# Weight tiles of the first stage put into the chain of loads, a gate tile between the fold and the first pooled tile, and the second pair's norms through the forms' buffers

## The chip, the cores and the metric

The kernel runs on one core of a Trainium2 chip. The metric is the device time of one execution in microseconds; before the change it is 656.79 us, the median of three runs (655.18 to 657.51).

## The reference, cut to what matters

One layer of a pooling mixer over 2048 rows of 1024 channels, all in float32:

```
hn     = rms_norm(x, norm_g)
proj   = hn @ pool_w_in                      # split: u (768) | mq (256) | gate (1024)
tok    = (causal means of u over windows 2, 4, 8, 16, per group of 192, minus u) @ w_group * pool_scale
mem_o  = 4-head attention of mq over rms_norm(mem, mem_norm_g) @ w_mem_kv   # 256 memory rows
h      = x + (concat[tok, mem_o] * silu(gate)) @ w_out
out    = rms_norm(h, final_norm_g)
```

## The kernel before

Rows are worked on in two pairs of blocks of 512 rows: `s = 0` and `s = 1`. Every float32 product is made of three matmuls of a rounded high part and a remainder (`_mm3`, lines 51 to 53), so each weight tile is first split: a cast on ScalarE writes the high part `wh` (line 38), and a subtraction on VectorE the remainder `wl` (line 46). The matrix of the group mixing is folded into the input projection on the chip: `fold` writes the product to `w_z` in DRAM, eight transfers from line 323.

The first stage (`s = 0`) goes through the tiles of the list `TILES`: "q" tiles are memory queries, "g" tiles the gate, "z" tiles the pooled channels, whose weights come from `w_z`. One tile over both blocks is 48 matmuls of 512 columns, in four runs of 12; after each run `tile_in` calls `between`, which is a step counter. At numbered steps it fires hooks: the two row norms of the first pair (7 and 10), the fold and the loads of the memory (12 and 14), the memory's keys and values (17), `stats(0)` and `stats(1)`, which compute the row norms of the second pair, and `stage(k)` at 25, 34, 43 and 52, which builds the seven combinations ("forms") of the second pair's inputs that the second stage multiplies (a Strassen-like scheme with seven products for eight). At eighteen other steps it does a piece of the memory attention of the first pair: scores (lines 580 and 581), exponentials (587), transposes of the probabilities (603), and the mix with the values (615).

`stats(a)` (`row_stats`) loads four tiles of rows of 512 KB, squares and sums them on ScalarE (line 220, two row tiles a line of the program), takes the power on GpSimd (line 200), spreads the result over a 128x512 tile (line 207), transposes that by four matmuls against the identity (209), copies it out of PSUM (210) and writes one row of it to `rows` in DRAM (253). `stage(k)` reads `rows` back, broadcast over the partitions, into two tiles `s` (259), and scales the inputs with them (266). In the kernel before, the two tiles in `row_stats` come from the pool `sg`, which has two buffers; the gate tiles use the same pool on their way to DRAM (`sg`, lines 497 and 498) and when a pooled tile reads them back (line 514). The pool `st`, name `s`, has two buffers too; in the first stage it serves the fold's small weights and then only `stage`.

A pooled tile ends in `windows`: GpSimd adds shifted copies (line 522), VectorE finishes and multiplies with the gate (531 to 537), and the result goes to `br_d` (539). All its tiles are from the pool `zz`, four buffers, which the fold, the memory and `x_later` use as well. `x_later` runs at the end of the first stage: it brings four of the seven forms back from DRAM (289) and splits them into the buffers that held the first pair's inputs.

The weight tiles are 512 KB each, in four buffers `raw`. The order of instructions on each engine is set when the program is built, by a scheduler that simulates the engines; each engine then works strictly through its own list. Loads issued through the helper `load` keep their written order on SyncE's queue; a plain `sp.dma_start` goes where the scheduler puts it. Transfers issued by SyncE and by ScalarE take one of eight semaphores (`DMAHW0` to `DMAHW7`) in turn, and the instruction that issues a transfer waits for the last one on the same semaphore.

Of the kernel before, what the change touches and what calls it, by code (L numbers as in the profile page):

```python
# [8 lines left out]
F32 = mybir.dt.float32  # L9
# [6 lines left out]
P = 128  # L16
# [4 lines left out]
BT = 512  # L21
NB = S // BT
QT = BT // P
# [25 lines left out]
def _mm3(nc, ps, ahi, alo, bhi, blo, start, stop, **kw):  # L49

    nc.tensor.matmul(ps, lhsT=ahi, rhs=bhi, start=start, stop=False, **kw)  # L51
    nc.tensor.matmul(ps, lhsT=ahi, rhs=blo, start=False, stop=False, **kw)  # L52
    nc.tensor.matmul(ps, lhsT=alo, rhs=bhi, start=False, stop=stop, **kw)  # L53
# [3 lines left out]
def trunk(ctx, tc, x, xT, mem, memT, norm_g, mem_norm_g, w_mem, w_out, w_in, w_uT, w_g, p_scale, final_g,  # L57
# [10 lines left out]
    st = pool("st", 2)  # L68
# [3 lines left out]
    sgp = pool("sgp", 2)  # L72
# [7 lines left out]
    def raw_tile(shape=(P, D)):  # L80
        return raw.tile(list(shape), F32, name="raw")
# [46 lines left out]
    def load_rows_of(b, slots, how):  # L128

        rows = []  # L130
        for i in range(QT):
            if i % 2 == 0:
                t = slot(slots[i // 2], (P, 2, D), F32)
            rows.append(t[:, i % 2, :])
            how(out=rows[i], in_=x[b * BT + i * P:b * BT + (i + 1) * P, :])
        return rows
# [9 lines left out]
    def load_tile(w, how=sp.dma_start):  # L146
        wr = raw_tile((P, KT, P))
        how(out=wr, in_=w)
        return wr
# [11 lines left out]
    ahead = [wq0, load_tile(w_in[1], load)]  # L161
# [34 lines left out]
    def rstd_of(ssq, n):  # L196
        v = small.tile([P, QT], F32, name="var")
        nc.vector.tensor_scalar(v[:, :n], ssq, 1.0 / D, EPS, ALU.mult, ALU.add)
        r = small.tile([P, QT], F32, name="rstd")
        nc.gpsimd.tensor_tensor(out=r[:, :n], in0=v[:, :n], in1=half[:, :n], op=ALU.pow)  # L200
        return r

    def bcast_cols(r, n, dst):

        ps = (ps_t if n == QT else ps_mm).tile([P, BT], F32, name="pt" if n == QT else "mm")
        rb = sgp.tile([P, BT], F32, name="sg")[:, :n * P].rearrange("p (t f) -> p t f", t=n)
        nc.vector.tensor_copy(rb, r[:, :n].unsqueeze(2).broadcast_to([P, n, P]))
        for t in range(n):
            nc.tensor.matmul(ps[:, t * P:(t + 1) * P], lhsT=rb[:, t, :], rhs=ident, start=True, stop=True)
        nc.vector.tensor_copy(dst, ps[:, :n * P])  # L210
# [6 lines left out]
    def squares(rows):  # L217
        ss = small.tile([P, QT], F32, name="ss")
        for t in range(QT):
            nc.scalar.activation(out=rows[t], in_=rows[t], func=AF.Square, accum_out=ss[:, t:t + 1])  # L220
        return rstd_of(ss, QT)
# [26 lines left out]
    def row_stats(s, a, rows):  # L248

        r = load_rows_of(2 * s + a, (10 + 2 * a, 11 + 2 * a), load)  # L250
        rb = sgp.tile([P, BT], F32, name="sg")
        bcast_cols(squares(r), QT, rb)
        sp.dma_start(out=rows[a].rearrange("(o t) p -> o (t p)", o=1), in_=rb[0:1])

    def stage_forms(s, k, rows, X):
# [39 lines left out]
    w_z = dram.tile([NJ, P, KT, P], F32, name="w_z")  # L295
# [58 lines left out]
    def memory_norm(loaded):  # L354
        ssm = small.tile([P, 2], F32, name="ssm", bufs=1)
        for t in range(2):
            nc.scalar.activation(out=loaded[1][t], in_=loaded[1][t], func=AF.Square, accum_out=ssm[:, t:t + 1])
        loaded.append(rstd_of(ssm, 2))
# [44 lines left out]
    def chunk(src, hi_eng, shape=(P, BT), lo_eng="dve"):  # L403

        hi = ch.tile(list(shape), F32R, name="wh")
        lo = ch.tile(list(shape), F32R, name="wl")
        _split(nc, hi, lo, src, hi_eng, lo_eng)
        return hi, lo
# [48 lines left out]
    def tile_in(xs, wr, ws, take, between):  # L457


        ps = {a: ps_mm.tile([P, BT], F32, name="mm") for a in xs}  # L460
        for kh in range(2):
            if len(ws) <= kh:
                ws.append(chunk(wr[:, kh * KH:(kh + 1) * KH], "act", (P, KH, P)))
            hi, lo = ws[kh]
            for a, hl in xs.items():
                for k in range(KH):
                    _mm3(nc, ps[a], hi[:, k, :], lo[:, k, :], hl[kh][0][:, k, :], hl[kh][1][:, k, :], k + kh == 0,
                         kh == 1 and k == KH - 1)
                between()
        for a in xs:  # L470
            def scaled(a=a):
                take(0, a, ps[a], ALU.mult, norms[a])
            if a in norms:
                scaled()
            else:
                unscaled[a].append(scaled)
# [14 lines left out]
    def take_gate(s, j):  # L491
        def take(i, a, ps, op, rest):
            sg = sgp.tile([P, BT], F32, name="sg")
            if rest is not None:
                nc.vector.tensor_tensor(out=sg, in0=ps, in1=rest, op=op)
                ps = sg
            nc.scalar.activation(out=sg, in_=ps, func=AF.Silu)
            nc.scalar.dma_start(out=g_d[s][j + i, :, a, :], in_=sg)
        return take
# [226 lines left out]
    loaded = []  # L726
# [15 lines left out]
    def tile_of(s, kind, j, xs, between):  # L742
        if kind == "q":
            tile_in(xs, ahead[j], qws[j], take_query(s, j), between)
        elif kind == "g":
            tile_in(xs, ahead[7 - j] if j > 3 and j < 6 else load_tile(w_in[2 + j]), [], take_gate(s, j), between)
        else:
            tile_in(xs, load_tile(w_z[j]), [], take_pool(s, j), between)

    qws = [[], []]  # L750
    state = {}
# [2 lines left out]
    def stats(a):  # L754
        if not a:
            load(out=ci, in_=cinv)
            state["rows"] = dram.tile([2, QT, P], F32, name="rows")
        row_stats(1, a, state["rows"])

    def stage(k):  # L760
        if not X1:
            X1.update(x_slots((1, 6, 2)))
        stage_forms(1, k, state["rows"], X1)


    TILES = [("q", 0, (0,)), ("q", 1, (0,)), ("q", 0, (1,)), ("q", 1, (1,))]
    TILES += [(kind, j, (0, 1)) for kind, j in (("g", 5), ("g", 4), ("z", 5), ("g", 3), ("z", 4), ("g", 2), ("z", 3), ("g", 1),
                                                ("z", 2), ("g", 0), ("z", 1), ("z", 0), ("g", 6), ("g", 7))]

    def norm(a):  # L770
        first_norm(a)
        for f in unscaled[a]:
            f()

    hooks = {7: [lambda: norm(0)], 10: [lambda: norm(1)], 12: [fold, lambda: ahead.append(load_tile(w_in[6], load)), lambda: loaded.extend(load_memory())],
             14: [lambda: load_memory_rest(loaded)],
             15: [lambda: memory_norm(loaded)], 17: [lambda: memory(loaded)], 18: [lambda: stats(0)], 21: [lambda: stats(1)]}
    for k in range(KH):
        hooks[25 + 9 * k] = [lambda k=k: stage(k)]
    steps = Steps(0, 20, 2.5, hooks)  # L780
    xs = {0: first_block(0)}
    for kind, j, blocks in TILES:
        if 1 in blocks and 1 not in xs:
# [91 lines left out]
```

## Time and profile before

| | us |
|---|---|
| median of three runs | 656.79 |
| the profiled execution's own time | 654.72 |
| its span | 652.9 |
| TensorE busy with matmuls | 602.1 (92%) |
| VectorE busy | 408.8 (63%) |
| ScalarE busy | 326.9 (50%) |
| GpSimd busy | 152.7 (23%) |
| mean granted TensorE clock, share of full speed | 0.964 |

The page of the profile lists busy time and cuts the span into 40 slices. The timeline lists single instructions: start, duration, engine, line, what it writes and reads, and in brackets the idle time before it with what ended it. SPq and ACTq are the queues by which SyncE and ScalarE issue transfers. Matmuls overlap in the pipeline, so at full clock one of 512 columns is listed with 0.39 us and the next starts 0.23 us later.

### The profile page before, as it was taken

What the parts mean: (1) busy time and instruction counts of PE and PEld (TensorE: products, weight loads), DVE (VectorE), ACT (ScalarE), POOL (GpSimd) and SP (SyncE); (2) the same over time, 40 slices, a digit from 0 to 9 for tenths busy, and PEclk for the clock granted to TensorE, in tenths of its full rate; (3) what the DMA queues carried; (4) which work ended last, traced back from release to release, by engine and by line L of the source; (5) the groups of instructions that cost most, each with busy time, mean ns of one, the idle gap of its engine ahead of it and who ended that gap; (6) DMA issues with size and microseconds to landing.
All of it is one profiled execution on the core that took longest, in us unless ns stands there. A gap on an engine that the chain in (4) does not pass through costs nothing.

```text
span 652.9 us, 8411 instructions
## 1 busy us (share of the span) xinstructions
PE 602.1 (92%) x2846; PEld 500.7 (77%) x2846; DVE 408.8 (63%) x686; ACT 326.9 (50%) x674; POOL 152.7 (23%) x165
## 2 busy tenths in 40 slices
PE   8999619996999999999999899989999999999993
PEld 5789519884887788888888687868888888888882
DVE  6370314658878977687769866898883337615126
ACT  6735450435647574765864689742752324214112
POOL 0021022806150413000018400364000002206016
PEclk8999959996999999999999899998999999999998
DMA  8949990318668545656340732256894046950006
GB/s 317 400 154 333 402 353 20 107 42 261 227 212 293 204 173 185 203 174 207 119 146 8 234 122 99 94 188 216 318 406 178 32 148 216 358 214 0 1 0 258
DMA packets 54382, 124.41 MB, mean 191 GB/s; under 512 B 6722, under 2 KB 15682, under 8 KB 54340
## 3 DMA queue, kind: packets, MB, share of 16 engines
q1 hardware_dynamic: 45972, 106.57, 47.0%
q10 hardware_dynamic: 6832, 12.60, 5.2%
q0 software_dynamic: 1536, 4.72, 1.9%
q8 instruction: 22, 0.36, 0.2%
q14 instruction: 20, 0.16, 0.1%
HBM read 86.63 MB, written 36.70 MB: 189 GB/s over the span
## 4 chain that ended last, share of the span: by engine, by line
PE 66%; DVE 11%; DMA 8%; ACT 8%; issue 4%; SPq 1%; POOL 1%; ACTq 0%; POOLq 0%; DVEq 0%
PE mm L51 16%; PE mm L53 15%; PE mm L52 15%; PE sc L51 2%; PE sc L52 2%; PE pt L51 2%; PE pt L52 2%; PE sc L53 2%; PE pt L53 2%; DVE wl L46 2%; DVE zz L537 2%; ACT L587 2%; ACT pr L587 1%; PE sc L615 1%; DMA x<-in_x 1%
## 5 line engine op out<-in xcount | busy, mean ns | idle before, releaser
L51 PE MATMUL mm<-x,wh 128*128 128x512 f32 x480 | 191.4, 401 | 26.2 <-ACT wh L38 20.2
L52 PE MATMUL mm<-x,wh 128*128 128x512 f32 x480 | 190.4, 397 | 0.3 <-DVE x L229 0.3
L53 PE MATMUL mm<-x,wl 128*128 128x512 f32 x480 | 188.6, 398 | 0.1
L46 DVE TENSOR_TENSOR wl<-raw,wh 128x512 fp32r<-128x512 f32 x104 | 79.3, 767 | 102.7 <-ACT wh L38 100.8
L38 ACT CAST wh<-raw 128x512 fp32r<-128x512 f32 x104 | 63.5, 618 | 128.6 <-PE pt L53 74.2
L51 PEld LDWEIGHTS mm<-x,wh 128*128 128x128 f32 x480 | 92.1, 192 | 46.1 <-ACT wh L38 20.9
L522 POOL TENSOR_TENSOR zz<-zz 128x527 f32<-128x527 f32 (+6 forms) x64 | 82.2, 1297 | 162.0 <-ACT zz L547 78.0
L52 PEld LDWEIGHTS mm<-x,wh 128*128 128x128 f32 x480 | 92.2, 192 | 18.8 <-DVE x L229 0.6
L53 PEld LDWEIGHTS mm<-x,wl 128*128 128x128 f32 x480 | 91.8, 191 | 19.1 <-DVE wl L46 0.9
L52 PE MATMUL mm<-wl,x 128*128 128x512 f32 x128 | 49.8, 389 | 0.0
L51 PE MATMUL mm<-wh,x 128*128 128x512 f32 x128 | 49.6, 389 | 0.0
L53 PE MATMUL mm<-wh,x 128*128 128x512 f32 x128 | 49.6, 389 | 0.0
L674 POOL TENSOR_TENSOR rstdo<-sso,half 128x1 f32<-128x1 f32 x16 | 14.7, 919 | 129.6 <-DVE sso L716 129.6
L587 ACT ACTIVATE pr<-sc,nm 128x256 f32<-128x256 f32 x64 | 29.7, 470 | 22.3 <-DVE nm L583 16.4
L592 ACT ACTIVATE pr<-pr,rc 128x256 f32<-128x256 f32 x64 | 29.0, 502 | 11.0 <-DVE rc L590 10.5
L38 ACT CAST pth<-pt 128x512 fp32r<-128x512 f32 x32 | 18.7, 585 | 19.0 <-PE pt L603 14.2
L51 PEld LDWEIGHTS mm<-wh,x 128*128 128x128 f32 x128 | 24.0, 188 | 5.1
L52 PEld LDWEIGHTS mm<-wl,x 128*128 128x128 f32 x128 | 24.0, 188 | 5.0
L53 PEld LDWEIGHTS mm<-wh,x 128*128 128x128 f32 x128 | 24.0, 188 | 4.9
L38 ACT CAST x<-zz 128x512 fp32r<-128x512 f32 x32 | 18.2, 618 | 14.7 <-DMA zz<-br_d 7.1
L52 PE MATMUL sc<-wl,x 128*128 128x512 f32 x64 | 24.9, 389 | 0.0
L53 PE MATMUL sc<-wh,x 128*128 128x512 f32 x64 | 24.9, 389 | 0.0
(177 smaller groups left out, 1049.8 us busy)
## 6 DMA issues: line engine op xcount, KB each, us to landing
raw<-in_w_in SPq DMA_DIRECT2D x19, 512.0 KB, 4.9
x<-in_x SPq DMA_DIRECT2D x16, 512.0 KB, 8.7
g_d<-sg ACTq DMA_DIRECT2D x32, 256.0 KB, 2.9
raw<-in_w_out SPq DMA_DIRECT2D x16, 512.0 KB, 4.4
raw<-w_z SPq DMA_DIRECT2D x12, 512.0 KB, 3.9
sg<-g_d SPq DMA_DIRECT2D x24, 256.0 KB, 3.1
br_d<-zz SPq DMA_DIRECT2D x12, 512.0 KB, 3.5
x<-in_xT SPq DMA_DIRECT2D x8, 512.0 KB, 7.2
```

The lines of the kernel that those rows point to most:

```text
L38: return nc.scalar.copy(hi, src)
L46: return e.tensor_tensor(out=lo, in0=src, in1=hi.bitcast(F32), op=ALU.subtract)
L51: nc.tensor.matmul(ps, lhsT=ahi, rhs=bhi, start=start, stop=False, **kw)
L52: nc.tensor.matmul(ps, lhsT=ahi, rhs=blo, start=False, stop=False, **kw)
L53: nc.tensor.matmul(ps, lhsT=alo, rhs=bhi, start=False, stop=stop, **kw)
L522: nc.gpsimd.tensor_tensor(out=cur[rows, c0:c1], in0=prev[rows, c0:c1], in1=prev[rows, c0 - step:c1 - step], op=ALU.add)
L537: nc.vector.scalar_tensor_tensor(out=v, in0=v, scalar=psc[:, j:j + 1], in1=gates[a], op0=ALU.mult, op1=ALU.mult)
L587: nc.scalar.activation(out=pr[:, h, :], in_=ps[:, h, :], func=AF.Exp, bias=nm[:, h:h + 1], accum_out=su[:, h:h + 1])
L592: nc.scalar.mul(pr[:, h, :], pr[:, h, :], rc[:, h:h + 1])
L615: nc.tensor.matmul(ps[:, h, :], lhsT=vhl[:, kt, p, h, :], rhs=part[:, n, :], start=kt == 0 and part is th, stop=kt == 1 and part is tl)
L674: nc.gpsimd.tensor_tensor(out=ro, in0=sso[:, 1, t:t + 1], in1=half[:, :1], op=ALU.pow)
```

## The change

Three parts. First, the weights of the first stage's gate and pooled tiles (`tile_of`) are loaded through `load` instead of the plain `sp.dma_start`. Second, the list `TILES` gets gate tile 3 ahead of the first pooled tile 5, and the following ones move so that each pooled tile stands one tile later; gate tile 6 moves ahead of pooled tiles 1 and 0. The hook `stats(0)` goes from step 18 to 19, and the eighteen attention steps start at 21 and come every 2.4 steps instead of at 20 and every 2.5. Third, `row_stats` takes its two tiles from the pool `st` (name `s`) instead of `sg`; `bcast_cols` gets an argument for that.

```diff
-    def bcast_cols(r, n, dst):
+    def bcast_cols(r, n, dst, rb=None):
...
-        rb = sgp.tile([P, BT], F32, name="sg")[:, :n * P].rearrange("p (t f) -> p t f", t=n)
+        rb = (sgp.tile([P, BT], F32, name="sg") if rb is None else rb)[:, :n * P].rearrange("p (t f) -> p t f", t=n)
...
     def row_stats(s, a, rows):
...
-        rb = sgp.tile([P, BT], F32, name="sg")
-        bcast_cols(squares(r), QT, rb)
+        rb = st.tile([P, BT], F32, name="s")
+        bcast_cols(squares(r), QT, rb, st.tile([P, BT], F32, name="s"))
...
-            tile_in(xs, ahead[7 - j] if j > 3 and j < 6 else load_tile(w_in[2 + j]), [], take_gate(s, j), between)
+            tile_in(xs, ahead[7 - j] if j > 3 and j < 6 else load_tile(w_in[2 + j], load), [], take_gate(s, j), between)
         else:
-            tile_in(xs, load_tile(w_z[j]), [], take_pool(s, j), between)
+            tile_in(xs, load_tile(w_z[j], load), [], take_pool(s, j), between)
...
-    TILES += [(kind, j, (0, 1)) for kind, j in (("g", 5), ("g", 4), ("z", 5), ("g", 3), ("z", 4), ("g", 2), ("z", 3), ("g", 1),
-                                                ("z", 2), ("g", 0), ("z", 1), ("z", 0), ("g", 6), ("g", 7))]
+    TILES += [(kind, j, (0, 1)) for kind, j in (("g", 5), ("g", 4), ("g", 3), ("z", 5), ("g", 2), ("z", 4), ("g", 1), ("z", 3),
+                                                ("g", 0), ("z", 2), ("g", 6), ("z", 1), ("z", 0), ("g", 7))]
...
-             15: [lambda: memory_norm(loaded)], 17: [lambda: memory(loaded)], 18: [lambda: stats(0)], 21: [lambda: stats(1)]}
+             15: [lambda: memory_norm(loaded)], 17: [lambda: memory(loaded)], 19: [lambda: stats(0)], 21: [lambda: stats(1)]}
...
-    steps = Steps(0, 20, 2.5, hooks)
+    steps = Steps(0, 21, 2.4, hooks)
```

What this makes of the instruction lists is shown at four places. First, SyncE's queue, from the last load of the memory's weights (`ptl<-in_w_mem`) on; `x<-in_x` are the rows of the second pair, `w_z<-zz` the last store of the fold, `raw` a weight tile, `mq` the attention's queries. Before:

```order
L123 DMA ptl<-in_w_mem 128x1024
L123 DMA ci<-in_cinv 128x96
L323 DMA w_z<-zz 128x6x128
L123 DMA x_958<-in_x 128x1024 x2
L123 DMA x_961<-in_x 128x1024 x2
L123 DMA x_1079<-in_x 128x1024 x2
L123 DMA x_1082<-in_x 128x1024 x2
L574 DMA mq<-q_d_174 64x512
L575 DMA mq<-q_d_174 64x512
L574 DMA mq<-q_d_174 64x512
L575 DMA mq<-q_d_174 64x512
L148 DMA raw<-w_z 128x1024
```

Now, at the same place of the same queue:

```order
L123 DMA ptl<-in_w_mem 128x1024
L123 DMA raw<-in_w_in 128x1024
L323 DMA w_z<-zz 128x6x128
L123 DMA ci<-in_cinv 128x96
L123 DMA x_974<-in_x 128x1024 x2
L123 DMA x_977<-in_x 128x1024 x2
L574 DMA mq<-q_d_174 64x512
L575 DMA mq<-q_d_174 64x512
L574 DMA mq<-q_d_174 64x512
L575 DMA mq<-q_d_174 64x512
L123 DMA raw<-w_z 128x1024
L123 DMA x_1059<-in_x 128x1024 x2
```

The tile after gate tile 4 is now gate tile 3, whose weights go out right behind the memory's; the weights of pooled tile 5 go out behind four of the eight row tiles.

Second, ScalarE at the end of gate tile 4, with the semaphores that each instruction waits for; 497 and 498 are the gate's SiLU and its store, 220 the squares of the second pair's rows, and the cast is the first one of the next tile's weights. Before:

```order
L498 DMA g_d_170<-sg 128x512 [waits DMAHW0_49,Activation_49]
L497 ACTIVATE sg<-sg 128x512 [waits DVE_49]
L498 DMA g_d_170<-sg 128x512 [waits DMAHW3_49,Activation_49]
L220 ACTIVATE x_958,ss<-x_958 128x1024 [waits DMAHW6_49]
L220 ACTIVATE x_958,ss<-x_958 128x1024 [waits DMAHW7_49]
L220 ACTIVATE x_961,ss<-x_961 128x1024
L220 ACTIVATE x_961,ss<-x_961 128x1024 [waits DMAHW1_49]
L220 ACTIVATE x_1079,ss<-x_1079 128x1024 [waits DMAHW2_49]
L220 ACTIVATE x_1079,ss<-x_1079 128x1024
L220 ACTIVATE x_1082,ss<-x_1082 128x1024 [waits DMAHW4_49]
L220 ACTIVATE x_1082,ss<-x_1082 128x1024 [waits DMAHW5_49]
L38 CAST wh<-raw 128x512 [waits DMAHW4_49,Pool_49]
```

Now:

```order
L498 DMA g_d_170<-sg 128x512 [waits DMAHW5_49,Activation_49]
L497 ACTIVATE sg<-sg 128x512 [waits DVE_49]
L498 DMA g_d_170<-sg 128x512 [waits DMAHW0_49,Activation_49]
L38 CAST wh<-raw 128x512 [waits DMAHW4_49,Pool_49]
L220 ACTIVATE x_974,ss<-x_974 128x1024 [waits DMAHW7_49]
L220 ACTIVATE x_974,ss<-x_974 128x1024
L220 ACTIVATE x_977,ss<-x_977 128x1024 [waits DMAHW1_49]
L220 ACTIVATE x_977,ss<-x_977 128x1024 [waits DMAHW2_49]
L220 ACTIVATE x_1059,ss<-x_1059 128x1024 [waits DMAHW2_49]
L38 CAST wh<-raw 128x512 [waits DVE_49,PE_49]
L220 ACTIVATE x_1059,ss<-x_1059 128x1024 [waits DMAHW3_49]
L38 CAST wh<-raw 128x512 [waits DMAHW1_49,DVE_49,PE_49]
```

The cast stands ahead of all squares, and the two stores of the gate take the semaphores of other transfers: before, of the third and the sixth row tile; now, of the fold's last store and of the second row tile.

Third, SyncE's queue where the second pair's norms go to DRAM and come back; `sg<-g_d` are the gates of a pooled tile. Before:

```order
L514 DMA sg<-g_d_170 128x512
L253 DMA rows<-sg 1x512
L514 DMA sg<-g_d_170 128x512
L259 DMA s<-rows 128x512
L539 DMA br_d_168<-zz 128x1024
L253 DMA rows<-sg 1x512
L259 DMA s<-rows 128x512
L514 DMA sg<-g_d_170 128x512
```

Now:

```order
L253 DMA rows<-s 1x512
L514 DMA sg<-g_d_170 128x512 x2
L259 DMA s<-rows 128x512
L253 DMA rows<-s 1x512
L259 DMA s<-rows 128x512
L123 DMA raw<-w_z 128x1024
L259 DMA s<-rows 128x512
L123 DMA raw<-in_w_in 128x1024
```

Block 1's row of norms no longer stands behind the store of the first pooled tile (`br_d<-zz`).

Fourth, TensorE at the first mix of the attention; `pt<-ident,pr` are the transposes of one or two score tiles, `mm` the projection. Before:

```order
L53 MATMUL mm<-x_264,wl 128x512
L603 MATMUL pt<-ident,pr 128x128 x8
L615 MATMUL sc<-pth,vhl 128x256
L580 MATMUL sc<-khi,mq 128x256
L581 MATMUL sc<-klo,mq 128x256
L580 MATMUL sc<-khi,mq 128x256
L581 MATMUL sc<-klo,mq 128x256
L615 MATMUL sc<-ptl,vhl 128x256
```

Now:

```order
L53 MATMUL mm<-x_176,wl 128x512
L603 MATMUL pt<-ident,pr 128x128 x4
L615 MATMUL sc<-pth,vhl 128x256
L580 MATMUL sc<-khi,mq 128x256
L581 MATMUL sc<-klo,mq 128x256
L580 MATMUL sc<-khi,mq 128x256
L615 MATMUL sc<-ptl,vhl 128x256
```

Before, the second and third score tile are transposed right ahead of the mix that needs the second; now the second is transposed 18 projection matmuls earlier, and only the third stands there. The transposes of block 1's norms stood 68 rows further down TensorE's list before (row 511) than now (row 443).

## Rows read from the trace of the kernel before

**Rows 1.** TensorE's waits: line, releaser: us in total, times, longest.
```profile
PE mm L51 <- ACT wh L38: 20.2, 1, 20.2
PE sc L615 <- DVE ptl L46: 4.4, 3, 2.4
```
**Rows 2.** Stretches: busy us (count) PE, PEld, DVE, ACT, POOL; clock; DMA share, GB/s.
```profile
75.00:96.00 21.00, 0.78 (x4) 0.32 (x3) 3.25 (x10) 11.78 (x23) 1.35 (x2) 0.62 1.01 374
...
147.00:162.00 15.00, 8.61 (x31) 6.32 (x30) 12.71 (x19) 8.16 (x18) 10.98 (x13) 0.66 0.82 270
162.00:200.00 38.00, 38.00 (x190) 32.05 (x189) 31.94 (x53) 21.18 (x47) 12.06 (x15) 1.00 0.67 221
200.00:220.00 20.00, 17.56 (x83) 13.70 (x82) 16.60 (x29) 13.50 (x25) 4.77 (x7) 1.00 0.67 230
```
**Rows 3.** The chain that ended last, 67 to 97 us: start, us, what.
```profile
69.61 8.08 DMA ptl<-in_w_mem
...
77.70 8.74 DMA x<-in_x
...
86.52 0.33 ACTq L498
```
**Rows 4.** ScalarE's timeline around the first gap: start, us, instruction, idle before.
```profile
82.75 0.33 ACTq L498 DMA_DIRECT2D g_d<-sg  x1
83.12 0.63 ACT L497 ACTIVATE sg<-sg 128x512 f32<-128x512 f32 x1 [5.66 <-DMA x<-in_x]
...
86.89 1.06 ACT L220 ACTIVATE x<-x 128x1024 f32<-128x1024 f32 x1 [3.15 <-DMA x<-in_x]
...
95.22 0.60 ACT L38 CAST wh<-raw 128x512 fp32r<-128x512 f32 x1
```
**Rows 5.** DMA issues of the page: KB each, median us to landing.
```profile
raw<-in_w_in SPq DMA_DIRECT2D x19, 512.0 KB, 4.9
x<-in_x SPq DMA_DIRECT2D x16, 512.0 KB, 8.7
...
br_d<-zz SPq DMA_DIRECT2D x12, 512.0 KB, 3.5
```
**Rows 6.** TensorE's timeline: behind the first gap, then the second stretch.
```profile
95.87 0.80 PE L51 MATMUL mm<-x,wh 128*128 128x512 f32 x1 [20.22 <-ACT wh L38]
...
100.05 0.63 PE L53 MATMUL mm<-x,wl 128*128 128x512 f32 x1
100.47 0.47 PE L51 MATMUL mm<-x,wh 128*128 128x512 f32 x1
...
101.24 0.39 PE L51 MATMUL mm<-x,wh 128*128 128x512 f32 x1
101.47 0.40 PE L52 MATMUL mm<-x,wh 128*128 128x512 f32 x1
...
148.16 0.84 PE L603 MATMUL pt<-ident,pr 128*128 128x128 f32 x4 [1.00 <-ACT pr L592]
149.54 0.38 PE L615 MATMUL sc<-pth,vhl 128*128 128x256 f32 x1 [0.55 <-ACT pth L38]
...
151.96 0.58 PE L615 MATMUL sc<-ptl,vhl 128*128 128x256 f32 x1 [1.56 <-DVE ptl L46]
...
157.02 0.58 PE L580 MATMUL sc<-khi,mq 128*128 128x256 f32 x1 [3.19 <-DMA sg<-g_d]
...
161.65 0.59 PE L52 MATMUL mm<-x,wh 128*128 128x512 f32 x1
```
**Rows 7.** SyncE's queue: the two rows of norms leave for DRAM.
```profile
123.84 0.31 SPq L253 DMA_DIRECT2D rows<-sg  x1
...
144.03 0.24 SPq L253 DMA_DIRECT2D rows<-sg  x1
```
**Rows 8.** VectorE and ScalarE at the end of the first stage.
```profile
260.32 1.41 DVE L537 SCALAR_TENSOR_TENSOR zz<-zz,psc,sg 128x512 f32<-128x512 f32 x2
...
274.68 2.18 ACT L38 CAST x<-zz 128x512 fp32r<-128x512 f32 x4
...
285.67 0.58 ACT L441 COPY u<-mm 128x512 f32<-128x512 f32 x1
```

## The prediction

> **What bounds the kernel now.** I read the page first: TensorE is busy for 602.1 of 652.9 us, so the kernel is its list of matmuls, and a change that neither adds nor removes any can only touch the 51 us in which it stands idle and the stretches at low clock. Next I read its waits [rows 1]. One of 20.2 us is far the longest; the others are of some 3 us and less, as in [rows 6]. Then I read busy time by stretch [rows 2]. The reader is to see two bad places: 75 to 96 us, where TensorE works for 0.78 us out of 21, and 147 to 162 us, where it is idle for 6.4 of 15 us and the granted clock is 0.66. Between and behind them it is full (38.00 of 38.00 us from 162 to 200), with 2.4 us missing from 200 to 220.
>
> The chain that ended last says why it stood still in the first gap [rows 3]. The load of the memory's last weights lands at 69.61 + 8.08 = 77.69; only then is the sixth row tile of the second pair issued, which lands at 86.44. ScalarE's second store of gate 4 waits for that landing and goes out at 86.52. Behind it, eight squares of 1.06 us begin at 86.89, and only then comes the cast of the next tile's weights, at 95.22 [rows 4]. None of this is work for the tile that TensorE waits for. It stands ahead of it in ScalarE's list.
>
> **The first gap, worked out.** In the new list the cast stands ahead of all squares; what is left ahead of it are the two stores. The first now waits for the fold's last store, the second for the second row tile. When does that land? The queue is full there (DMA share 1.01, 374 GB/s [rows 2]), so I count bytes. Before, the first store went out at 82.75 [rows 4], when the third row tile had landed: behind the load that ended at 77.69 came the fold's store (384 KB) and three row tiles of 512 KB. Now come gate 3's weights (512 KB), the same store and two row tiles. That is the same number of bytes, so I expect the second store at 82.75 too. From the second store to the first square it was 86.89 - 86.52 = 0.37 us, and from the start of the cast to the first matmul 95.87 - 95.22 = 0.65 us [rows 4, 6]. TensorE starts at 82.75 + 0.37 + 0.65 = 83.8 instead of 95.9: 12.1 us gained, 8.2 us of the gap are left.
>
> The ends for this term. If row tiles land as late as before (second store at 86.52), the start is at 87.5 and 8.3 us are gained. If only the first 512 KB behind 77.69 count, at the rate of those bytes (1.9 MB in 5.06 us, about 1.35 us a tile), the cast starts at 79.1, the matmul at 79.7, and 16.2 us are gained. I take 12.1.
>
> The clock. Behind the gap the matmuls come every 0.42 us (100.05, 100.47) and later every 0.23 (101.24, 101.47) [rows 6]; from 95.87 to 100.47 about half of 4.6 us, 2.3 us, is lost. In the second stretch the clock was lost after idle times of 1.0, 0.55, 1.56 and 3.19 us in a row, so I expect 8.2 us to lose it as well: no gain here, 2.3 us if the clock holds.
>
> A rule of the Trainium skill sees this otherwise ("DMA: Bandwidth & Descriptors", section "Anatomy of one DMA"): a transfer costs about 2.0 us fixed and its bytes at 436 GB/s, fitted on GpSimd's path. By it 512 KB take an estimated 3.2 us. The rows say 8.7 us for a row tile and 4.9 for a weight tile, medians [rows 5], because transfers queue. What the rule would give is the third rival below.
>
> What is queued behind the cast: the squares of the second block's rows, spread between the casts of the next tiles. They end later than before relative to the cast, but their result is first needed by the transposes of block 1's norms, which stand 35 rows of TensorE's list behind those of block 0 and at least 7 us of matmuls after them (33 projection matmuls at 0.23 us). The memory's casts on GpSimd no longer stand behind the powers of the norms, so they are ready when TensorE starts. The first pooled tile's weights go out behind four row tiles and wait for the third of them: some 84 us, a landing near 88, while gate 3 and the memory's matmuls keep TensorE in the same amount of work as pooled tile 5 and the memory did before, 95.87 to 122 = 26 us. They cost nothing; without that cover they would cost about 4 us.
>
> **The second stretch, worked out.** Idle 1.00 + 0.55 + 1.56 + 3.19 = 6.3 us [rows 6]. At low clock: seven matmuls of 256 columns behind 151.96, 0.1 us too long each, 0.7 us, and half of 157.02 to 161.65 and a little more, 2.4 us. In all 9.4 us. The cause is one of order: block 1's norms leave for DRAM only at 144.03, twenty us after block 0's at 123.84 [rows 7], since they needed a `sg` buffer that the first pooled tile's gates held; their PSUM bank held up the transposes of the second score tile, and three attention steps were put on one spot of TensorE's list, where each waits for ScalarE and VectorE in turn, whose forms start at the same time. With the norms in `s` their transposes stand 68 rows earlier, the second score tile is transposed 18 matmuls (4.1 us) ahead of the mix, and the norms return about 24 us sooner (12 from the first gap, the rest from the order). I leave 2.0 us: the mix still stands four instructions ahead of the one that needs `ptl`, which cost 1.56 us before, and something near 0.5 us beside it; without the longer idle times the clock stays. Gain 7.4 us. The ends: nothing, or 3 us worse, if VectorE, busy for 12.7 of 15 us there and 31.9 of 38 behind, is what all this waits for; 9.4 and the 2.4 us from 200 to 220 as well, 11.8 us, if the attention runs free.
>
> **The end of the first stage.** Pooled tile 0 now has one tile behind it instead of two, 48 x 0.227 = 10.9 us less. Its last VectorE work ended at 261.7 before [rows 8]; 10.9 us later is 272.6, and with 3.5 us for the store (the median for `br_d<-zz` [rows 5]) its `zz` buffers are free at 276. Form 7, the second that `x_later` brings back, needs them, then a load and the casts that started at 274.68 [rows 8]: say 281. The first product of the second stage is evacuated at 285.67 [rows 8], so that stage starts near 282.9, and form 7 is its fifth product, at 282.9 + 4 x 12 x 0.227 = 293.8. Some 12 us of cover; cost nothing. The `load` helper itself only fixes the order of weight tiles among themselves and costs nothing: the issues are the same in number. The second stage and the output stage have the same instructions; their small waits may come out 3 us either way, about one wait like the 3.19 at 157.02 [rows 6].
>
> **Sum.** 654.72 - 12.1 - 7.4 = 635.2 for an execution like the profiled one, which is 2.1 us under the median shown. On the scale of the median that is **637.3, so 637 us**; its own range is 632 to 642.
>
> **The rivals.**
> 1. Only the first gap shrinks. The second stretch is bound by VectorE's forms and ScalarE's exponentials, and moved as a whole it stays 6 to 9 us long. For it: VectorE is at 84% in the 38 us behind. Against: those 38 us show no TensorE idle at that load. Time 656.8 - 12.1 = 645 (641 to 649).
> 2. No change: the time gained is given back where the next list is late, in the forms or the attention, because the chain that ended last runs through VectorE and ScalarE from 143 to 220 us. It would need 17 us of new waits where 11 stood. Time 655 to 658.
> 3. The transfers land fast, by the mechanism of the skill's fit above: without a queue ahead of them the second row tile is there 3.2 us after its issue near 73, the store goes out at 76.5, TensorE starts at 77.5 and never loses the clock: 18.4 + 2.3 + 7.4 = 28.1 us gained, time 629. Against it stand all eight row tiles of this stretch.
> 4. Slower: the second stage starves. Pooled tile 0's buffers come free so late that form 7 or 5 isn't there when its product is due, because `windows`, the casts of `x_later` and the attention's last steps all ask VectorE at once. TensorE's wait has to be over 19.5 us to turn the sign, that is form 7 ready after 313 on the scale of before instead of 281. Time 658 to 664 with a wait of 21 to 27 us. The cover of 12 us speaks against it.
>
> **How the numbers follow.** The forecast has 0.60, rival 1 0.25, rival 2 0.05, rival 3 0.03, rival 4 0.07. What a measurement of this kernel can tell from no change is 0.3%, about 2 us. Forecast, rivals 1 and 3 are faster: 0.88. Of rival 2 most is within 0.3%, 0.04; the rest and rival 4 make 0.08 slower. For 8 in 10 the range takes in the forecast's own with the ends of both terms and rival 1 to its far end: 630 to 649.
>
> **What would show it.** Right: one TensorE wait of about 8 us for ScalarE's cast near 76 to 84 us, ScalarE's store released near 82.75, squares behind the cast; block 1's norms leaving near 119; no idle of over 2 us from 110 to 160 and the granted clock at 1.00 there; no wait at the first form products. Wrong: a wait above 12 us in the first gap; TensorE waits in front of lines 580 and 615 that still add up to 6 us; waits of the second stage for `x` at the casts of forms 5 or 7.

## The result, and the profile after

The changed kernel takes 635.0 us, the median of four runs (634.29 to 636.03), against 656.38 for the kernel before (655.18 to 657.51, four runs). The ratio is 0.968, 95% interval 0.965 to 0.970: faster by 3.0 to 3.5%. The profiled execution of the changed kernel took 636.03 us, the slowest of its four, with a span of 634.3; that of the kernel before, with 654.72, was a little faster than the four. So the two profiles differ by 18.7 us and the medians by 21.4. The working below goes by the profiles.

TensorE's waits after the change, in the columns of [rows 1]:

```profile
PE mm L51 <- ACT wh L38: 8.3, 1, 8.3
PE sc L615 <- DVE ptl L46: 4.2, 4, 2.7
PE pt L603 <- ACT pr L592: 3.9, 4, 2.8
PE mm L51 <- ACT sg L497: 1.7, 2, 1.3
```

The wait of 20.2 us is 8.3 now. It is still the longest, still for ScalarE's cast at line 38. The waits of the attention (lines 603 and 615) have not gone. The stretches, in the columns of [rows 2], show the same: TensorE works again from 84 us on, but 122 to 147 and 162 to 200, which had been full, now miss 2.7 and 3.5 us and are granted 0.93 and 0.96 of the clock. A stretch of the same times holds later work than before, since all of it comes some 12 us sooner. The first line is of the kernel before, the others of the changed one:

```profile
122.00:147.00 25.00, 25.00 (x128) 21.11 (x126) 13.14 (x24) 9.60 (x22) 10.25 (x11) 1.00 0.18 60
```

```profile
75.00:84.00 9.00, 0.73 (x2) 0.50 (x2) 1.19 (x2) 3.91 (x8) 0.62 (x1) 0.67 1.05 393
84.00:101.00 17.00, 17.00 (x116) 15.99 (x115) 10.42 (x22) 7.63 (x15) 4.45 (x7) 0.88 0.91 294
122.00:147.00 25.00, 22.31 (x103) 18.59 (x102) 24.12 (x32) 11.27 (x29) 12.86 (x14) 0.93 0.60 194
147.00:162.00 15.00, 14.65 (x77) 12.28 (x76) 13.91 (x21) 8.59 (x16) 8.57 (x10) 1.00 0.64 213
162.00:200.00 38.00, 34.49 (x159) 27.36 (x157) 25.89 (x44) 19.32 (x43) 13.63 (x17) 0.96 0.59 204
200.00:220.00 20.00, 18.80 (x90) 15.09 (x90) 17.63 (x33) 13.43 (x28) 6.97 (x10) 1.00 0.66 228
```

ScalarE's timeline at the end of gate tile 4, which answers to [rows 4]:

```profile
79.77 0.33 ACTq L498 DMA_DIRECT2D g_d<-sg  x1
80.14 0.63 ACT L497 ACTIVATE sg<-sg 128x512 f32<-128x512 f32 x1 [3.05 <-DMA w_z<-zz]
82.38 0.33 ACTq L498 DMA_DIRECT2D g_d<-sg  x1
82.80 0.62 ACT L38 CAST wh<-raw 128x512 fp32r<-128x512 f32 x1 [2.04 <-DMA x<-in_x]
83.33 1.05 ACT L220 ACTIVATE x<-x 128x1024 f32<-128x1024 f32 x1
```

The first store waits for the fold's last store, the second for a row tile that took 8.01 us from 74.29. The cast follows 0.42 us behind the second store, and the squares come after the cast.

To say where the 18.6 us of span went I use one point that both programs pass with the same work done: ScalarE's copy of the second stage's first product (line 441). Up to it, both traces show the same number of matmuls on each line of the attention (64 of line 615, 32 of 580, 64 of 603), 36 transposes of line 209, and counts on lines 51 to 53 that agree within one. Before, it starts at 285.67 ([rows 8]); after, here:

```profile
272.33 0.59 ACT L441 COPY u<-mm 128x512 f32<-128x512 f32 x1
```

| part of the span | before | after | gain | forecast |
|---|---|---|---|---|
| to TensorE's start behind the first gap | 95.87 | 83.47 | 12.4 | 12.1 |
| from there to the copy of the first product | 189.8 | 188.9 | 0.9 | 7.4 |
| from that copy to the end of the span | 367.2 | 362.0 | 5.3 | 0, 3 either way |

The total was forecast well because one term was too large and another, set at nothing, made up for most of what was missing.

In the runs below the first copy does not always stand at the same place: 1234 to 1251 matmuls have started ahead of it, and 14 matmuls are some 3 us. Where it matters I count to the start of the matmul behind the first 1250 of each trace instead (each trace has 2846). By that count the change gained 1.5 us in the second row of the table (192.9 to 191.4) and 4.8 in the third (364.2 to 359.4).

### The profile page after: what moved, and what is told of

It is laid out like the page before. It is cut to its first block, busy times and chain, and to the rows that moved or that the text cites. A ratio compares the mean times of both kernels' runs of the same rounds, so it can differ in the third digit from the quotient of the medians.

```text
span 634.3 us, 8389 instructions
## 1 busy us (share of the span) xinstructions
PE 598.7 (94%) x2846; PEld 496.6 (78%) x2846; DVE 406.2 (64%) x686; ACT 324.9 (51%) x672; POOL 153.7 (24%) x165
## 4 chain that ended last, share of the span: by engine, by line
PE 62%; DVE 14%; DMA 7%; ACT 6%; POOL 5%; issue 4%; SPq 1%; ACTq 0%; POOLq 0%; DVEq 0%
PE mm L51 14%; PE mm L52 14%; PE mm L53 14%; POOL zz L522 4%; DMA raw<-in_xT 3%; PE sc L52 2%; PE sc L53 2%; PE pt L52 2%; PE pt L53 2%; PE pt L51 2%; PE sc L51 2%; DVE wl L46 2%; PE mm L317 2%; DVE raw L101 2%; DVE zz L531 1%
## 5 line engine op out<-in xcount | busy, mean ns | idle before, releaser
L46 DVE TENSOR_TENSOR wl<-raw,wh 128x512 fp32r<-128x512 f32 x104 | 76.7, 741 | 110.8 <-ACT wh L38 110.5
L522 POOL TENSOR_TENSOR zz<-zz 128x527 f32<-128x527 f32 (+6 forms) x64 | 84.5, 1332 | 145.7 <-DVE zz L549 48.7
L38 ACT CAST x<-raw 128x512 fp32r<-128x512 f32 x28 | 16.8, 619 | 21.7 <-DVE raw L266 13.9
L46 DVE TENSOR_TENSOR x<-raw,x 128x512 fp32r<-128x512 f32 x28 | 23.6, 864 | 4.1 <-ACT x L38 3.9
L583 DVE TENSOR_REDUCE nm<-sc 128x2 f32<-128x512 f32 x32 | 21.8, 682 | 5.2 <-PE sc L581 5.0
```

What stands on the lines that cost most here:

```text
L38: return nc.scalar.copy(hi, src)
L46: return e.tensor_tensor(out=lo, in0=src, in1=hi.bitcast(F32), op=ALU.subtract)
L522: nc.gpsimd.tensor_tensor(out=cur[rows, c0:c1], in0=prev[rows, c0:c1], in1=prev[rows, c0 - step:c1 - step], op=ALU.add)
L583: nc.vector.tensor_reduce(out=nm, in_=ps, axis=AX.X, op=ALU.max, negate=True)
```

## The experiments

The three parts of the change are called load (weights in the chain of loads), order (list of tiles and steps) and norms (the second pair's norms through `s`). All seven combinations ran, each beside the kernel before; the columns are those of the table above, with the gap itself, and in the last one the time from the 1250th matmul to the end.

| parts | median, us | ratio to before, 95% | first gap | start behind it | start to first copy | copy to end | 1250th to end |
|---|---|---|---|---|---|---|---|
| none | | | 20.22 | 95.87 | 189.8 | 367.2 | 364.2 |
| load | 644.82 | 0.979 to 0.985 | 8.09 | 84.71 | 191.1 | 367.5 | 364.2 |
| order | 632.19 | 0.963 to 0.968 | 0.54 | 76.64 | 187.6 | 367.6 | 366.0 |
| norms | 650.97 | 0.990 to 0.995 | 19.39 | 95.74 | 184.8 | 365.8 | 362.8 |
| load, norms | 637.90 | 0.972 to 0.980 | 7.28 | 83.16 | 185.7 | 366.4 | 362.7 |
| order, norms | 632.26 | 0.964 to 0.969 | 0.44 | 76.50 | 191.9 | 361.5 | 359.5 |
| load, order | 634.10 | 0.966 to 0.971 | 7.91 | 83.58 | 184.7 | 363.2 | 359.6 |
| all three | 635.00 | 0.965 to 0.970 | 8.27 | 83.47 | 188.9 | 362.0 | 359.4 |

**Order and norms, without load.** The changed kernel with:

```diff
-            tile_in(xs, load_tile(w_z[j], load), [], take_pool(s, j), between)
+            tile_in(xs, load_tile(w_z[j]), [], take_pool(s, j), between)
```

and the same for the gate tiles.

> The changed kernel with the weights of the first stage loaded by the plain transfer again. In this list gate 3's weights go out on SyncE's queue three transfers earlier, ahead of the fold's last two stores and of the memory's last two weight tiles, and ScalarE's cast stands ahead of both stores of gate 4. Theory A (the first gap lasts as long as ScalarE's stores wait for a landing, and the weights themselves are there earlier): the 8.3 us gap shrinks to 0 to 3 us and the clock is not lost, 635 - 6 to 10 = 625 to 629. Rival B (the chain of loads is what shortened the gap, since it keeps row tiles away from the weights): a gap of 12 to 20 us, 639 to 647. Rival C (the queue is full, so whatever goes ahead makes the memory's weights late by as much): the gap gets short but TensorE waits as long in the memory's products, 633 to 637.

632.26 us, between A's range and C's. A was right on the gap (0.44 us) and wrong on the total: part of it came back, as C had said, but not from late weights. TensorE's waits of over 2 us behind the gap:

```profile
88.02 0.80 PE L53 MATMUL sc<-zz,wl 128*128 128x256 f32 x2 [3.55 <-DVE wl L46]
136.07 0.58 PE L615 MATMUL sc<-ptl,vhl 128*128 128x256 f32 x1 [4.97 <-DVE ptl L46]
181.68 0.84 PE L603 MATMUL pt<-ident,pr 128*128 128x128 f32 x4 [3.21 <-ACT pr L592]
```

The first is in the memory's products. ScalarE's cast now stands ahead of the store, but its scaling of the memory (line 368) stands behind it, and VectorE's list goes on to `wl` only behind that:

```profile
84.71 0.33 ACTq L498 DMA_DIRECT2D g_d<-sg  x1
85.14 1.70 ACT L368 ACTIVATE zz<-mq,gm 128x256 fp32r<-128x256 f32 x4 [8.69 <-DMA x<-in_x]
```

The store holds back whatever is next in the list. The run of order alone with these stores on GpSimd's queue, below, bears this out.

**Load and norms, without order.** The old list of tiles and the old steps; of the edit, the last line:

```diff
...
-    steps = Steps(0, 21, 2.4, hooks)
+    steps = Steps(0, 20, 2.5, hooks)
```

> The changed kernel with the old list of tiles and the old steps: pooled tile 5 follows gate 4, loads in the chain, norms through `s`. ScalarE's cast stands ahead of the squares here too, but the weights of pooled tile 5 can only be read back when the fold's last store has landed (79.7 us in the changed kernel's trace), so they land near 84. Theory A (what counts is the place of the cast): TensorE starts near 84.5 to 86, a first gap of 9 to 11 us, second stretch somewhat better than before, 640 (636 to 647). Rival B (the gate tile between is what shortens the first gap): the gap stays at 16 to 20 us and the time at 649 to 656.

637.90 us: A in the total; the gap of 7.28 us is shorter than A's 9 to 11. A gate tile between is not needed to shorten the gap.

**Load and order, without norms.** Of the edit, one pair of lines:

```diff
...
-        rb = st.tile([P, BT], F32, name="s")
+        rb = sgp.tile([P, BT], F32, name="sg")
...
```

> The changed kernel with the second pair's norms in the gates' buffers `sg` as before. With the new list of tiles the transposes of block 1's norms do not stand late in TensorE's list even so (row 437 against 443 with the change and 511 before). Theory A (the norms were late because of the list of tiles, the buffers only add to it): 633 to 639, like the changed kernel. Rival B (the buffers are what moved the norms and the second stretch): the second stretch is as before, 641 to 645.

634.10 us: A. The interval of its ratio overlaps that of the whole change; no gain of the norms through `s` on top of the other two is shown. Its way from the gap to the first copy is 4.2 us shorter than with the norms in `s`, 3.1 by the 1250th matmul (188.3 against 191.4).

**Order alone.**

> The kernel before with the new list of tiles and steps alone: plain transfers, norms in `sg`. Cast and weights stand as early as without the chain of loads. Theory A (cast and weights early, no landing waited for): first gap 0 to 3 us, 625 to 631. Rival B (each of the three parts is needed): 640 to 650. Rival C (the time comes back in the memory's products or behind): 633 to 639.

632.19 us. The gap is gone, as A had it; the total is 1 us above A's range and just under C's. It started 6.8 us earlier than the whole change and reached the first copy 8.1 us earlier (264.28), but its second stage is 5.6 us longer. By the ratios it can't be told from the whole change.

**Norms alone and load alone.** The first tests whether the eight squares are what made the gap of 20 us, the second whether load by itself moves the cast.

> The kernel before with the second pair's norms through `s` alone. The cast stands behind the eight squares still, the transposes of block 1's norms stand 66 rows earlier in TensorE's list. Theory A (first gap from the place of the cast, second stretch from the norms' place): the first gap stays at 19 to 21 us, the second stretch loses 4 to 8 us, 647 to 651. Rival B (the second stretch is bound by VectorE's work, wherever the norms stand): 653 to 657.

> The kernel before with the weights of the first stage in the chain of loads and nothing else. ScalarE's cast stands ahead of the squares; the weights of pooled tile 5 go out when the fold's last store has landed. Theory A (the place of the cast is what counts, and any part of the change that moves it ahead of the squares closes most of the first gap): first gap 7 to 10 us, second stage as before, 637 to 643. Rival B (load and tile order are needed together): gap 16 to 20 us, 649 to 655.

Norms alone: 650.97 us, the gap stays at 19.39, and 5.0 us are gained from the gap to the first copy: A. Load alone: 644.82 us, 1.8 above A's range, gap 8.09 us as A had it. So the cast stands behind the squares in both lists with a gap of 19 and 20 us, and ahead of them in all others.

The place of the cast is not all that differs, though. Load and order also bring the weights sooner. In the kernel before, the weights of pooled tile 5 go out behind all eight row tiles, and land 5.1 us later, near 93.7:

```profile
88.57 0.34 SPq L148 DMA_DIRECT2D raw<-w_z  x1
raw<-w_z SPq DMA_DIRECT2D x1, 512.0 KB, 5.1
```

The cast began at 95.22. Put ahead of the squares, with nothing else changed, it could have come some 1.5 us sooner, as an estimate from these rows; no run has the one without the other. With load alone the same weights go out at 79.11, and it is for them, not for a store, that the cast waits:

```profile
84.04 0.62 ACT L38 CAST wh<-raw 128x512 fp32r<-128x512 f32 x1 [5.86 <-DMA raw<-w_z]
```

It is so with load and norms (82.49, a wait of 5.00 us for `w_z`). With the new list the tile is gate 3, whose weights do not come from the fold. So the gap ends with the later of two things: the weights of the next tile, and what stands ahead of its cast.

**Gate 4's stores from GpSimd's queue.** The changed kernel with:

```diff
-            nc.scalar.dma_start(out=g_d[s][j + i, :, a, :], in_=sg)
+            (nc.gpsimd if s == 0 and j == 4 else nc.scalar).dma_start(out=g_d[s][j + i, :, a, :], in_=sg)
```

> The changed kernel with the two stores of gate tile 4 issued from GpSimd's queue instead of ScalarE's, which take no semaphore of the other transfers. Order of ScalarE and SyncE otherwise as in the changed kernel. Theory A (the 8.3 us gap is ScalarE's list held by a store that waits for the second row tile, 82.38; gate 3's weights are there earlier): the cast starts when the weights land, at 77 to 80, the gap is 2 to 5 us, and the memory's products are not late: 628 to 632. Rival B (the weights land near 82 anyway, in a full queue): the wait stays and names the transfer instead, 634 to 637.

630.88 us (ratio 0.963, 0.958 to 0.968): A, though the interval still overlaps that of the changed kernel. ScalarE now waits for the weights themselves, which are there at 79.2, 3.6 us ahead of the changed kernel's cast:

```profile
77.64 0.61 ACT L497 ACTIVATE sg<-sg 128x512 f32<-128x512 f32 x1
79.22 0.62 ACT L38 CAST wh<-raw 128x512 fp32r<-128x512 f32 x1 [0.97 <-DMA raw<-in_w_in]
```

The gap is 3.85 us, and ends with the weights. The other 4.4 of the 8.3 us were a store standing in front.

**The same with order alone, with order and norms, and with load and order.**

> The kernel before with the new list of tiles and steps alone, and gate 4's two stores from GpSimd's queue. With the list alone the first gap was 0.5 us, but the memory's products then waited 2.9 us at 87.5, since ScalarE's scaling of the memory stood behind a store that waited for a row tile. Theory A (that store is what held the scaling): the 2.9 us go, 628 to 630. Rival B (the memory's weights are late by the 512 KB that went ahead of them): the wait stays, 632 to 634.

> New list of tiles and norms in `s`, plain loads, gate 4's stores from GpSimd's queue: gate 3's weights early, no store in ScalarE's list, so no first gap and no wait of the memory's products. Its second stage has the list of the kernel before, which was some 4 us longer in the runs so far (366 us from the first product to the end, against 362). Theory A (the length of the second stage hangs on its list, whatever the first stage does): second stage 365 to 367, total 629 to 633. Rival B (the second stage is short when the first one ends well): 361 to 363, total 625 to 628.

> Chain of loads and new list of tiles, norms in `sg`, gate 4's stores from GpSimd's queue. Its second stage has the same list as the changed kernel's. Theory A (the store is what held the cast; first and second stage add up): gap 3.5 to 4.5 us instead of 7.9, nothing given back, 629 to 631.5. Rival B (what the first gap gives is given back in the attention's waits): 632 to 635.

With order alone: 635.16 us, above A's range and B's, and by the medians 3.0 us slower than without, though the intervals (0.965 to 0.975 and 0.963 to 0.968) overlap. The memory's wait of 2.9 us went as A had said, but 1.62 us came at the norms of the memory (line 209), and in the attention three waits of 2.28 to 3.07 us stand where order alone has one of 2.19. With order and norms: 634.26 us, above A's total, though the second stage took 366.2 us as A had it; the first copy, at 266.42, is only 1.0 us earlier than in the run with 3.85 us of gap. With load and order: 631.32 us (ratio 0.961, 0.958 to 0.964), in A's range, gap 3.50 us; of the 3.7 us by which it starts sooner, 1.8 are left at the first copy (266.43). This last one is faster than the changed kernel by its interval, and has the lowest ratio of the versions run.

None of the four versions with a gap under 1 us has a lower median than the two with a gap near 4 us. Against the changed kernel with GpSimd's stores (first copy at 267.45) the lead was gone at the first copy in two of them (268.37 for order and norms, 270.08 for order with GpSimd's stores) and 1.0 us in a third; order alone kept 3.2 us of it (264.28), and lost more than that in its longer second stage.

**The additions of pooled tile 5 on VectorE.** The changed kernel's wait of 2.7 us at line 615 stands behind an odd row. VectorE and GpSimd:

```profile
133.37 0.68 DVE L46 TENSOR_TENSOR wl<-raw,wh 128x512 fp32r<-128x512 f32 x1
133.97 0.15 DVE L590 RECIPROCAL rc<-su 128x2 f32<-128x2 f32 x1
134.04 4.31 DVE L46 TENSOR_TENSOR x<-raw,x 128x512 fp32r<-128x512 f32 x1
138.28 0.68 DVE L46 TENSOR_TENSOR ptl<-pt,pth 128x512 fp32r<-128x512 f32 x1
```

```profile
134.30 3.49 POOL L522 TENSOR_TENSOR zz<-zz 128x512 f32<-128x512 f32 x3
```

One subtraction takes 4.31 us where its neighbour of the same shape takes 0.68, and ends 0.56 us behind GpSimd's third addition. `ptl`, for which TensorE waits, is the next in VectorE's list. The edit:

```diff
-                    nc.gpsimd.tensor_tensor(out=cur[rows, c0:c1], in0=prev[rows, c0:c1],
+                    (nc.vector if s == 0 and j == 5 else nc.gpsimd).tensor_tensor(out=cur[rows, c0:c1], in0=prev[rows, c0:c1],
...
```

> The changed kernel with the shifted additions of pooled tile 5 alone on VectorE instead of GpSimd: eight more instructions of some 0.6 us on VectorE between 125 and 145 us. In the changed kernel VectorE's subtraction for the input parts takes 4.31 us at 134 instead of 0.68, while GpSimd makes three of these additions, and TensorE waits 2.69 us at 139 for the instruction behind it. Theory A (a VectorE instruction that reads two SBUF tiles stands still while GpSimd reads): the long one is gone, all take under 1.3 us in that stretch, the wait at 139 is under 1 us, 631 to 634. Rival B (the duration has another cause, or the 5 us more of VectorE work cost as much): the wait is there or moves, 634 to 638.

The mechanism came out as A, the time did not. The same stretch:

```profile
134.01 0.68 DVE L46 TENSOR_TENSOR x<-raw,x 128x512 fp32r<-128x512 f32 x1
134.61 0.68 DVE L46 TENSOR_TENSOR ptl<-pt,pth 128x512 fp32r<-128x512 f32 x1
135.22 1.89 DVE L522 TENSOR_TENSOR zz<-zz 128x512 f32<-128x512 f32 x3
```

The long instruction is gone there, TensorE's wait too, and the first copy comes at 269.67 instead of 272.33, 2.7 us earlier. Another subtraction of the same shape takes 4.07 us at 183.12, beside additions that are still on GpSimd, and TensorE waits 2.46 us at 190. The total is 637.61 us, in B's range, because the second stage takes 365.9 us instead of 362.0: its list had changed nearly to the form that the kernel before has.

**The second stage's list.** Its length came in two sizes: 361.5 to 363.2 us with some lists, 365.8 to 367.6 with the others (363.8 once, with order alone and GpSimd's stores, where the first copy stands 14 matmuls further on than before; from the 1250th matmul on it takes 364.0 and belongs to the long ones, which take 362.7 to 366.0 by that count, the short ones 359.4 to 360.3). The last experiment leaves the first stage alone and moves only the attention in the second, on the version with GpSimd's stores:

```diff
-    project_in(1, X1, Steps(1, 10, 2, {NP - 4: [lambda: bring(0, 0, (0, 1, 2, 3), "zz")],
+    project_in(1, X1, Steps(1, 11, 2, {NP - 4: [lambda: bring(0, 0, (0, 1, 2, 3), "zz")],
...
```

> The changed kernel with gate 4's stores from GpSimd's queue, and the second pair's attention begun one step later in the second stage (11 instead of 10). The first stage has the same list. Theory A (the second stage's length hangs on where its attention steps fall among the products): the first stage ends within 1 us of the run without the shift (first product's copy at 267.5), the second stage changes by 1.5 to 6 us, either way. Rival B (its length is that of its matmuls and the few waits don't depend on the list): 630 to 632, second stage within 1 us of 362.6.

637.46 us, by the medians 6.6 us slower than without the shift: A. The profiled executions differ by 4.8 us. The first copies of the run without the shift and of the run with it:

```profile
267.45 0.59 ACT L441 COPY u<-mm 128x512 f32<-128x512 f32 x1
```

```profile
267.48 0.59 ACT L441 COPY u<-mm 128x512 f32<-128x512 f32 x1
```

The first stage is the same to 0.03 us; the second takes 367.5 instead of 362.7. TensorE's waits for VectorE's sums of products (`u`, line 104), without the shift and with it:

```profile
PE mm L51 <- DVE u L104: 1.2, 3, 0.6
```

```profile
PE mm L51 <- DVE u L104: 4.2, 2, 2.5
```

## Why the prediction was right, and where it was not

**What bounds the kernel, and the first gap: right.** The gap was forecast at 8.2 us and is 8.27; the second store at 82.75, and it went out at 82.38; TensorE's start at 83.8, and it was 83.47. The count of bytes in a full queue held. What the prediction said of the kernel before was only part of the cause: it named the squares ahead of the cast, but the weights themselves landed only some 1.5 us before it. For the new list this made no difference, since gate 3's weights were there (the cast could begin at 79.22 once the stores were off) and the store was last. The clock fell behind 8.27 us of idle time, granted 0.51 from 84 to 88.3 us and 1.00 from there to 101: no gain there, as forecast. The third rival is out with this: the row tile that released the store took 8.01 us.

**The second stretch: wrong.** The step that failed is the one by which late norms were the cause of its 9.4 us and the norms in `s` the cure. Block 1's norms did leave early:

```profile
109.62 0.31 SPq L253 DMA_DIRECT2D rows<-s  x1
...
117.84 0.24 SPq L253 DMA_DIRECT2D rows<-s  x1
```

That is 26 us sooner than before ([rows 7]), and 1 us off the forecast. But the 7.4 us did not follow: 0.9 us were gained between the gap and the first copy, 1.5 by the 1250th matmul. The table shows why. Norms alone gain 5.0 us there (189.8 to 184.8), and 5.4 on top of load (191.1 to 185.7), near the forecast. On top of the new list of tiles they cost 4.3 us (187.6 to 191.9) and 4.2 (184.7 to 188.9); by the 1250th matmul 4.6 and 3.1. I added two parts as if each worked alone. The new list alone had already moved block 1's norms. In the run with load and order they left at

```profile
119.73 0.24 SPq L253 DMA_DIRECT2D rows<-sg  x1
```

which is 1.9 us later than in the changed kernel. Their transposes begin with the 528th matmul of that trace, the 518th of the changed kernel's and the 582nd before; the rows 437 and 443 named ahead of that run do not fit this order.

What the norms cost on top of load and order is in the clock. The changed kernel, then the run without the norms part:

```profile
100.00:200.00 100.00, 93.46 (x449) 77.04 (x447) 75.94 (x122) 50.84 (x114) 40.50 (x49) 0.97 0.57 183
```

```profile
100.00:200.00 100.00, 93.18 (x463) 76.15 (x462) 80.56 (x132) 53.41 (x119) 40.80 (x50) 1.00 0.58 183
```

TensorE is idle for 6.5 and 6.8 us. In the changed kernel most of it is in two waits, of 2.69 us at 139 and 2.83 at 184, and behind each the granted clock is 0.50 for over 3 us:

```profile
139.50:142.80 3.30, 3.30 (x13) 2.82 (x12) 2.42 (x6) 1.47 (x3) 0.00 (x0) 0.50 0.90 280
183.90:187.10 3.20, 3.08 (x10) 2.49 (x11) 3.20 (x5) 2.79 (x6) 2.40 (x3) 0.50 0.63 159
```

In the other run the longest wait is 1.78 us and the clock stays at 1.00. Two such stretches at half speed are some 3.3 us, about the 3.1 that the norms cost. On top of order alone it is waits as well: 4.97 and 3.21 us in the attention, where order alone has one of 2.19.

The first of the two waits is explained. One subtraction of 4.31 us stands in front of `ptl`, and taking GpSimd's additions away gave 2.7 us back. Without the norms part VectorE meets GpSimd's additions as well, but `ptl` stands ahead of the subtraction:

```profile
132.51 0.67 DVE L46 TENSOR_TENSOR ptl<-pt,pth 128x512 fp32r<-128x512 f32 x1
133.10 2.13 DVE L46 TENSOR_TENSOR x<-raw,x 128x512 fp32r<-128x512 f32 x1
```

Why the second wait came, for ScalarE's `pr`, stays open. The sign I had written for no idle of over 2 us from 110 to 160 and a clock of 1.00 failed at 139:

```profile
139.01 0.38 PE L615 MATMUL sc<-ptl,vhl 128*128 128x256 f32 x1 [2.69 <-DVE ptl L46]
```

The bound of zero gain was in the range, and the first rival, which rested on it, was near the time of the first stage. Its reason does not hold as stated: norms alone have the same work for VectorE and ScalarE and gained 5.0 us, so the order of that work counts.

**The end of the first stage: right.** `x_later`'s casts ran from 257.26 to 272.3 and TensorE did not wait for them. The fourth rival fell with that.

**The second stage: mis-sized.** Set at nothing, with 3 us either way, it gave 5.3. TensorE's waits there fell from 5.2 us (2.35 and 2.83) to 2.4 (1.34, 0.63 and 0.39). The rest of the gain is in the clock. Before, it was granted at half behind each of the two waits; in the changed kernel it is 1.00 from 290 to 600 us. The first two lines are of before:

```profile
363.50:366.80 3.30, 3.30 (x10) 2.58 (x9) 3.30 (x6) 1.70 (x7) 2.10 (x2) 0.50 0.94 305
442.00:445.30 3.30, 3.30 (x10) 2.59 (x9) 1.31 (x3) 0.62 (x1) 0.00 (x0) 0.50 0.34 98
```

```profile
290.00:600.00 310.00, 306.80 (x1430) 253.49 (x1429) 196.74 (x321) 157.74 (x325) 67.95 (x52) 1.00 0.48 167
```

The two waits alone do not decide it: with norms alone they are as long (2.35 and 2.84 us), and the clock is 1.00 from 290 to 600 all the same. The list of the second stage changed although no line of the edit touches it, because the scheduler goes on from where the first stage leaves it. The shift by one step shows that such a change of list alone moves it by 4.8 us. Of the seven combinations those with order and load, norms or both got the shorter list, but order and norms with GpSimd's stores got the longer one; why, stays open.

So the first stage came out near the first rival, which gave 645 for the whole; the second stage made up for most of it. The forecast of 637 is right in its largest term and lucky in the sum of the other two.

## What to carry to other kernels

Two parts that cure the same lateness need not add; here one that gained 5 us alone cost 3 to 5 on top of the other. Ask of each what the other has already moved, and read it from the lists with one part left out. When a program's lists are made by a scheduler, compare the stages that the edit doesn't touch as well, and give them a term of several us, not nothing. When a wait is put down to what stands ahead in a list, read also when the data behind it landed: the two can end within 2 us of each other. An engine that issues a transfer can wait there for an earlier one, with all its list behind it: ScalarE's second store waited 2.04 us for a row tile, with the cast behind it. A store on the engine that feeds TensorE is to be looked at first.

## What the runs showed of the hardware that was not expected

A VectorE instruction that reads two tiles of SBUF stood still while GpSimd read: 4.31 us against 0.68 at 134.04, and 4.39 in the same place of the run with order and norms; 0.68 once GpSimd's additions were off. Both times it ended 0.56 us behind the third of three additions in a row. The Trainium skill says so ("SBUF — State Buffer", section "Who interferes with whom"): a VectorE instruction with two SBUF inputs contends with a GpSimd instruction that reads SBUF, and the shared ports are an exclusive lock, which the one that issues first holds for its whole instruction. The trace agrees on the blocking. Who issued first it does not show: VectorE's instruction is recorded 0.26 us before GpSimd's first addition and yet waited for three of them, but recorded starts on GpSimd are rough, and GpSimd was issuing a transfer from 133.74 to 134.28.
